# Turning mixing weights, head outputs and the normed context through the DMA's crossbar

## The chip, the core and the metric

The kernel runs on one core of one Trainium2 chip. The metric is the device time of one run in microseconds (us); before the change it is 1346.94 us, the median of three runs (1346.42 to 1347.75). The engines are TensorE (PE in the profile; its weight loads are PEld), VectorE (DVE), ScalarE (ACT), GpSimd (POOL) and SyncE (SP), which here only issues DMAs.

## The reference

The reference is a two-layer trunk over 256 context tokens and 256 latent tokens of width 1024, in float32. Layer 0 has a bidirectional chunkwise mLSTM as its token mixer, layer 1 a multi-head latent attention; behind each stands a gated feed-forward part with a convolution. Every part is modulated by the conditioning (scale and shift), and its output is added to the input and normed:

```python
h = x*(1+scale)+shift
x = LayerNorm(ALPHA*x + gate*sublayer(h))
# mLSTM of layer 0, 4 heads of 256 (q, k) and 512 (v), per direction and chunk:
wmat = jnp.exp(dmat - mj[..., None]) * jnp.einsum("bhjd,bhsd->bhjs", qc, kc)
num = g[..., None] * jnp.einsum("bhjd,bhde->bhje", qc, C) + jnp.einsum("bhjs,bhse->bhje", wmat, vc)
den = g * jnp.einsum("bhjd,bhd->bhj", qc, n) + jnp.sum(wmat, -1)
h = num / jnp.maximum(jnp.abs(den), jnp.exp(-mj))[..., None]
```

Each head's output is multiplied by an output gate, normed over its 512 columns (root mean square) and projected together with the others (the product called mout here).

## The kernel before, in words

**Matrix products.** A float32 product is made of three matmuls (`mm3`, lines 430, 433 and 434): each operand is split in a rounded high half, which ACT writes by a copy, and the remainder, its low half, which DVE writes by a subtraction (`split`, lines 444 and 445). The weights stream: SP loads 512 KB into `raw` (three buffers), ACT casts the high half of `w` (line 345), DVE subtracts for the low half (line 368), and PE multiplies from `w` (three buffers; some of the last weights of a product go to `wu`, from a larger pool).

**The mixer by heads.** Gates and all of v are there already: v in DRAM as `vd`, the output gates as `od`, the log decays as `ad`. For each head h from 0 to 3, `w_qk(h)` projects q and k (four column blocks of 128, each with 48 matmuls, and four casts `qk`), then `av(h-1)` multiplies the mixing weights of the head before with its v, and `s_mm(h)` makes the scores S of head h (`sc` and `sl` on PE, three copies `S` by ACT). Between the matmuls of `w_qk(h)` background generators advance a step at a time:

- `post(h-2)` norms the gated output `oh` of head h-2: four squares and a root on ACT, four scalings on DVE. Then PE turns the 16 blocks of 128x128 into `hnT` in PSUM, and ACT and DVE split each with its norm weight into `hn`.
- `head(h-1)` loads the decays of head h-1 over all partitions (`aB`, by POOL), adds the causal mask (`Am`, DVE), and makes the mixing weights W in three groups g of rows: exponentials on ACT, products with S, row sums and scalings on DVE. Then PE turns 12 blocks into `PT` in PSUM, and ACT and DVE split them.
- `v_load(h-1)`, called late in `w_qk(h)`, has POOL load v (`vr`) and the gate (`oh`), and has ACT and DVE split v.

A second background list computes the modulations of later parts (`ar` loads by SP, reductions on DVE of 1.2 us, called `junk` at line 544).

**mout and the norm.** After the loop mout runs over the 256 context tokens: the 16 blocks k of `hn` in turn, with `head(3)` and `post(2)` beside the first eight, then `av(3)`, then the others with `post(3)`. Its second pass, over the latent tokens, has the layer norm of the context rows beside it (`after0`): `ln_rows` norms two tiles `z` of 128x1024, and `ln_T` turns 16 blocks into `zT` in PSUM, modulates them (`zm`) and splits them into `h0`, the input of the feed-forward part.

**What sets the order.** The code's order, with the steps of the generators in between, is the starting point. When the kernel is built, a scheduler puts each engine's instructions in an order of its own, in which an instruction may pass others that it does not depend on; `behind` keeps an instruction after another one of its engine. A buffer is handed out from a pool (`s2`: 15 of 128x512, `u`: 31 of 128x1024), and the write into it waits until its former tile has been read. Each engine works through its list in order, so that an instruction that waits holds up everything behind it; SP and POOL issue DMAs in order, too.

Of the kernel before, what the change touches and what calls it, by code (L numbers as in the profile page):

```python
# [8 lines left out]
F32R = mybir.dt.float32r  # L9
I32 = mybir.dt.int32  # L10
AF = mybir.ActivationFunctionType
ALU = mybir.AluOpType
# [21 lines left out]
NB, NRAW, NU, NS = 3, 3, 31, 15  # L34
# [366 lines left out]
class K:  # L401
# [41 lines left out]
    def split(self, hi, lo, src):  # L443
        self.nc.scalar.copy(hi, src)
        self.nc.vector.tensor_sub(lo, src, hi)

    def smc(self, name):
# [593 lines left out]
    def head(self, h, S, big=False):  # L1041
        nc = self.nc
        aB = [self.s2("aB0"), self.s2("aB1")]
# [11 lines left out]
        P = []  # L1055
        for g in range(3):
            jbs = [0, 1] if g == 0 else [g + 1]
# [8 lines left out]
            for i, t in enumerate(jbs):  # L1066
                base = 256 * i if g == 0 else 0
                for d in range(2):
                    o = W[d]
                    bias = self.gcol[:, 0, t, 32 * d + h:32 * d + h + 1]  # L1070
# [28 lines left out]
            for i, t in enumerate(jbs):  # L1099
# [7 lines left out]
                                               op0=ALU.mult, op1=ALU.add)  # L1107
                P.append((W[big], b0))
            yield
        yield  # L1110
        self.PT = []
        for grp in ([(t, s) for s in range(2) for t in (0, 1)], [(t, s) for s in range(2) for t in (2, 3)],
                    [(t, s) for s in (2, 3) for t in (2, 3)]):
# [68 lines left out]

    def post(self, h, tt):
        nc = self.nc
# [6 lines left out]
        for t in range(4):  # L1191
            nc.vector.tensor_scalar(tt[t], tt[t], ss[:, t:t + 1], None, op0=ALU.mult)
        yield
        g = self.smc("mng")
        for e in range(4):
# [11 lines left out]
            self.hn[k] = u  # L1207
        yield


# [68 lines left out]
    def ln_T(self, zs, A, B, dst, tail, both=True, between={}):  # L1279

        nc = self.nc
        lone = both and tail
        for k0 in (0, 2, 6) if lone else range(0, 8, 2 if both else 4):
# [37 lines left out]
            for k in range(k0, k0 + n) if both else ():  # L1321
# [10 lines left out]
                if k % 2 or not tail:  # L1332
                    yield

    def aout_fin(self, o1, pl, xr, gate, fi, h1u, att):
# [846 lines left out]
def build(tc, off, a, out):  # L2182
    es = ExitStack()
    with es:
# [16 lines left out]
        tt = None  # L2201
        k.hn = {}
        for h in range(H0):
# [5 lines left out]
            if h >= 1:  # L2209
                gens.append(k.head(h - 1, S))  # L2210
            k.bg = gens
            k.w_qk(h, 2, (lambda: k.v_load(h - 1)) if h >= 1 else None)
# [6 lines left out]
        pc = k.acc4()  # L2219
        k.bg = [k.head(3, S, True), k.post(2, tt)]  # L2220
        vs = k.v_steps(3)
# [4 lines left out]
        tt = k.av(3)  # L2226
        k.bg = [k.post(3, tt)]
        k.outmm("mout", range(8, 12), hn, pc, 0, 16, 1, n2=ADA_M)
# [10 lines left out]
        def after0(pss, xr, gate, g, ln, l, c, dst, xdst):  # L2239
# [3 lines left out]
            zs = k.zs  # L2243
            yield from k.ln_T(zs, A, B, dst, g == 1)
            if xdst is not None:
# [117 lines left out]
```

## Time and profile before

| | before |
|---|---|
| median of three runs | 1346.94 us (1346.42 to 1347.75) |
| profiled execution: its span, the one time that its page gives | 1345.3 us |
| PE busy | 1334.9 us, 99% |
| DVE busy | 1059.0 us, 79% |
| ACT busy | 711.7 us, 53% |
| POOL busy | 141.5 us, 11% |
| chain of waits | 97% PE |
| DMA | 304.02 MB, mean 226 GB/s |

The span runs from the first to the last instruction that the profiler recorded. A row of the timeline gives start, duration, engine, line, operation, tile and inputs, and in brackets the idle time before it and who ended it. Rows of consecutive equal instructions are joined (x16): the duration is then that of all. A row of a tile's instructions gives the shortest, middle and longest duration in ns. A row of the DMA issues gives the size and the median time from issue to landing.

### The profile page before, as it was taken

Reading aid. Unit: us, or ns where it says so; the run is one execution under the profiler, and the core shown is the slowest. Engines: PE = TensorE matmul, PEld = TensorE weight load, DVE = VectorE, ACT = ScalarE, POOL = GpSimd, SP = SyncE. Lnnn points to the kernel's source line nnn. Section 1 sums busy time; section 2 is a strip of 40 time slices with the busy share of each in tenths; the row PEclk is TensorE's granted clock in tenths of the full one; section 3 lists DMA queues with packets and bytes.
Section 4 is the critical chain, followed back from the end, with each engine's and each line's share of the span. In section 5 each row is a group of like instructions: output and inputs, shape, how many; then the busy total and the mean of one; then the engine's idle time right before and its main releaser. Section 6 shows DMA issues by size and latency. Waiting matters only on the chain.

```text
span 1345.3 us, 18750 instructions
## 1 busy us (share of the span) xinstructions
PE 1334.9 (99%) x6659; PEld 1120.2 (83%) x6659; DVE 1059.0 (79%) x1745; ACT 711.7 (53%) x1252; POOL 141.5 (11%) x236
## 2 busy tenths in 40 slices
PE   9999999999999999999999999999999999999997
PEld 5777888888888888888898888888888998988886
DVE  4798656678688696897979977758899889898874
ACT  4765444445744546474644334333566767676660
POOL 0222000011101011020002011111000002000100
PEclk9999999999999999999999999999999999999999
DMA  9988848889686384776628989967866437376750
GB/s 364 330 277 279 281 163 248 233 272 307 235 281 230 102 255 149 228 292 222 215 86 261 328 260 286 282 181 184 300 223 194 157 104 219 127 212 189 263 189 32
DMA packets 99885, 304.02 MB, mean 226 GB/s; under 512 B 12312, under 2 KB 25112, under 8 KB 99712
## 3 DMA queue, kind: packets, MB, share of 16 engines
q1 hardware_dynamic: 62992, 218.65, 48.6%
q0 software_dynamic: 26000, 66.75, 17.9%
q10 hardware_dynamic: 10800, 17.44, 3.6%
q8 instruction: 52, 0.85, 0.3%
q14 instruction: 41, 0.34, 0.1%
HBM read 272.21 MB, written 42.12 MB: 234 GB/s over the span
## 4 chain that ended last, share of the span: by engine, by line
PE 97%; DMA 1%; DVE 1%; ACT 0%; issue 0%; SPq 0%; DVEq 0%; ACTq 0%
PE fin L1503 8%; PE tok L430 6%; PE tok L434 6%; PE tok L433 6%; PE fin L433 6%; PE fin L434 6%; PE y L433 6%; PE fin L430 6%; PE y L434 6%; PE y L430 6%; PE qk L430 4%; PE qk L433 4%; PE qk L434 4%; PE up L718 2%; PE up L430 2%; PE up L434 1%
## 5 line engine op out<-in xcount | busy, mean ns | idle before, releaser
L368 DVE TENSOR_TENSOR w<-raw,w 128x1024 fp32r<-128x1024 f32 (+2 forms) x286 | 343.2, 1203 | 131.9 <-ACT w L345 129.7
L345 ACT CAST w<-raw 128x1024 fp32r<-128x1024 f32 (+2 forms) x286 | 296.2, 1037 | 282.4 <-PE tok L434 77.8
L544 DVE SCALAR_TENSOR_TENSOR junk<-ar,bc 128x1024 f32<-128x1024 f32 x128 | 156.1, 1219 | 5.2 <-ACT bc L586 2.3
L433 PE MATMUL fin<-h,w 128*128 128x512 f32 (+1 forms) x370 | 139.6, 377 | 0.0
L430 PE MATMUL fin<-h,w 128*128 128x512 f32 (+1 forms) x370 | 139.5, 377 | 0.0
L434 PE MATMUL fin<-h,w 128*128 128x512 f32 (+1 forms) x370 | 139.3, 377 | 0.0
L1503 PE MATMUL fin<-h,w 128*128 128x512 f32 (+1 forms) x636 | 111.1, 337 | 0.0
L1503 PEld LDWEIGHTS fin<-h,w 128*128 128x128 f32 x636 | 97.6, 190 | 13.2
L430 PE MATMUL qk<-xc,w 128*128 128x512 f32 x256 | 100.2, 391 | 0.0
L434 PE MATMUL qk<-xc,w 128*128 128x512 f32 x256 | 99.8, 390 | 0.0
L433 PE MATMUL qk<-xc,w 128*128 128x512 f32 x256 | 99.6, 389 | 0.0
L433 PEld LDWEIGHTS fin<-h,w 128*128 128x128 f32 x370 | 69.6, 188 | 13.0
L430 PEld LDWEIGHTS fin<-h,w 128*128 128x128 f32 x370 | 69.6, 188 | 12.9
L434 PEld LDWEIGHTS fin<-h,w 128*128 128x128 f32 x370 | 69.6, 188 | 12.6
L434 PEld LDWEIGHTS qk<-xc,w 128*128 128x128 f32 x256 | 48.0, 188 | 10.1
L430 PEld LDWEIGHTS qk<-xc,w 128*128 128x128 f32 x256 | 48.1, 188 | 9.8
L433 PEld LDWEIGHTS qk<-xc,w 128*128 128x128 f32 x256 | 48.1, 188 | 9.8
L430 PE MATMUL tok<-w,hT 128*128 128x512 f32 x128 | 49.9, 390 | 0.0
L433 PE MATMUL tok<-w,hT 128*128 128x512 f32 x128 | 49.8, 389 | 0.0
L434 PE MATMUL tok<-w,hT 128*128 128x512 f32 x128 | 49.8, 389 | 0.0
L735 ACT ACTIVATE fg<-fg 128x512 f32<-128x512 f32 (+1 forms) x44 | 23.1, 525 | 50.0 <-DVE fg L733 43.9
L368 DVE TENSOR_TENSOR wu<-raw,wu 128x1024 fp32r<-128x1024 f32 (+1 forms) x37 | 43.8, 1203 | 3.5 <-ACT wu L345 3.2
(486 smaller groups left out, 3125.7 us busy)
## 6 DMA issues: line engine op xcount, KB each, us to landing
raw<-in_ws SPq DMA_DIRECT2D x282, 512.0 KB, 4.5
ar<-in_adaT SPq DMA_DIRECT2D x80, 512.0 KB, 6.0
t4d<-in_ws POOLq DMA_DIRECT2D x20, 512.0 KB, 9.1
adaw<-in_ada SPq DMA_DIRECT2D x16, 512.0 KB, 8.0
zr<-fd ACTq DMA_DIRECT2D x33, 128.0 KB, 4.6
xmd<-xr POOLq DMA_DIRECT2D x16, 256.0 KB, 4.4
xcd<-cv POOLq DMA_DIRECT2D x16, 256.0 KB, 4.9
xs<-xmd POOLq DMA_DIRECT2D x16, 256.0 KB, 6.0
```

The costliest lines, as they stand in the source:

```text
L345: self.cast = k.nc.scalar.copy(h[:, :cols], src)
L368: i = self.k.nc.vector.tensor_sub(l[:, :n], src, h[:, :n])
L430: q = mm(out, w[0], x[0], start=start, stop=False, skip_group_check=on)
L433: mm(out, w[0], x[1], start=False, stop=False, skip_group_check=on)
L434: mm(out, w[1], x[0], start=False, stop=stop, skip_group_check=on)
L544: nc.vector.scalar_tensor_tensor(o, w, 1.0, self.bc[j], op0=ALU.mult, op1=ALU.mult, accum_out=col[:, k, j:j + 1])
L718: nc.tensor.matmul(ps[m], wk[i][:, c], hT[k][:, j], start=made[m] == 0, stop=made[m] == 23)
L735: nc.scalar.activation(tmp[:, :n], tmp[:, :n], AF.Silu)
L1503: self.nc.tensor.matmul(ps[:, 0:256] if x else ps, w[x][:, k * 128:(k + 1) * 128], h[:, 0:256] if x else h, start=i == 0 and not k0, stop= ...
```

## The change

For heads 0 to 2 the blocks of W and of `oh`, and for the context rows those of `z`, are no longer turned on PE. ACT copies a tile into `pl` with the two 16-bit halves of each float32 in separate planes (`planes`), POOL writes `pl` to DRAM (`pd`, `hd`, `zd`), and SP issues transposing DMAs of 16-bit elements that read it and leave the turned float32 block in SBUF (`px`, `hx`, `zx`, 256 KB each). ACT and DVE then split from there. In numbers: 36 PE transposes of W, 48 of `oh` and 16 of `z` go; 26 copies on ACT, 26 writes by POOL and 25 transposing DMAs on SP come. `turn_heads`, a generator of its own, takes what `post` left in DRAM, one head later in the loop. Head 3 and the latent rows keep the PE transposes.

```diff
+    def planes(self, dst, src):
+        i = self.nc.scalar.copy(dst, src.bitcast(U16).rearrange("p (n h) -> p h n", h=2))
+        return i
...
     def head(self, h, S, big=False):
-        nc = self.nc
+        nc, last = self.nc, big
+        pd = None if last else self.dr.tile([512, 2, 512], U16, name="pd")
...
                 P.append((W[big], b0))
+            if not last:
+                n = 256 if g == 0 else 512
+                pl = self.pool.tile([128, 2, 512], U16, tag="s2", name="pl", bufs=NS)
+                for i, t in enumerate(jbs):
+                    p = pl if g else pl.rearrange("p a (b n) -> p (a b) n", b=2)[:, 2 * i:2 * i + 2]
+                    src, b0 = P[t]
+                    self.planes(p, src[:, b0:b0 + n])
+                    nc.gpsimd.dma_start(pd[t * 128:(t + 1) * 128, :, 0:n], p)
             yield
         yield
         self.PT = []
+        if not last:
+            v = pd.rearrange("t h n -> (t h) n")
+            for t0, s0 in ((0, 0), (2, 0), (2, 2)):
+                x = self.s2("px")
+                nc.sync.dma_start_transpose(x.bitcast(U16).rearrange("p (s t) -> p s t", s=2),
+                                            v[256 * t0:256 * t0 + 512, 128 * s0:128 * s0 + 256])
+                u = self.u("PT")
+                self.split(u[:, 0], u[:, 1], x)
+                self.PT.append(u)
+            yield
+            return
...
-    def post(self, h, tt):
+    def post(self, h, tt, last=False):
...
+        if not last:
+            d = self.dr.tile([512, 2, 512], U16, name="hd")
+            for t in range(4):
+                pl = self.pool.tile([128, 2, 512], U16, tag="s2", name="pl", bufs=NS)
+                self.planes(pl, tt[t])
+                nc.gpsimd.dma_start(d[t * 128:(t + 1) * 128], pl)
+            self.turned.append((h, d))
+            yield
+            return
...
+    def turn_heads(self):
+        nc, g = self.nc, self.smc("mng")
+        h, d = self.turned.pop(0)
+        v = d.rearrange("t h n -> (t h) n")
+        xs = []
+        for e in range(4):
+            x = self.s2("hx")
+            nc.sync.dma_start_transpose(x.bitcast(U16), v[:, e * 128:(e + 1) * 128])
+            xs.append(x)
+            if e % 2:
+                yield
+        for e in range(4):
+            k, x = h * 4 + e, xs[e]
+            u = self.u("hn")
+            nc.scalar.activation(u[:, 0], x, AF.Copy, scale=g[:, k:k + 1])
+            nc.vector.scalar_tensor_tensor(u[:, 1], x, g[:, k:k + 1], u[:, 0], op0=ALU.mult, op1=ALU.subtract)
+            self.hn[k] = u
...
+    def ln_turn(self, zs, A, B, dst):
+        nc = self.nc
+        d = self.dr.tile([256, 2, 1024], U16, name="zd")
+        for t in range(2):
+            pl = self.pool.tile([128, 2, 1024], U16, tag="u", name="pl", bufs=NU)
+            self.planes(pl, zs[t])
+            nc.gpsimd.dma_start(d[t * 128:(t + 1) * 128], pl)
+            pl = None
+            yield
+        v = d.rearrange("t h n -> (t h) n")
+        xs = []
+        for k in range(0, 8, 2):
+            x = self.s2("zx")
+            nc.sync.dma_start_transpose(x.bitcast(U16).rearrange("p (k t) -> p k t", k=2), v[:, 128 * k:128 * k + 256])
+            xs.append(x)
...
+            nc.scalar.activation(m, m, AF.Identity, bias=B[:, k:k + 1], scale=A[:, k:k + 1])
+            hi, lo = dst(k)
+            nc.scalar.copy(hi, m)
+            nc.vector.tensor_sub(lo, m, hi)
...
             if h >= 1:
                 gens.append(k.head(h - 1, S))
+            if h >= 2:
+                gens.append(k.turn_heads())
...
-    k.bg = [k.head(3, S, True), k.post(2, tt)]
+    k.bg = [k.head(3, S, True), k.post(2, tt), k.turn_heads()]
...
-            yield from k.ln_T(zs, A, B, dst, g == 1)
+            if g:
+                yield from k.ln_T(zs, A, B, dst, True)
+            else:
+                yield from k.ln_turn(zs, A, B, dst)
```

The new work also moves instructions that the diff does not name. The first piece is ACT's list in the second half of `w_qk(2)`, before the change, from the cast of the first `PT` of head 1 on; `vr` is v as loaded, `adav` a column of the background modulations.

```order
L444 CAST PT_4174<-PT_4169 128x512
L444 CAST PT_4182<-PT_4177 128x512
L444 CAST PT_4190<-PT_4185 128x512
L559 COPY adav_78<-w_4198 1x1
L444 CAST qk_4233<-qk_4139 128x512
L444 CAST v_4239<-vr_4237 128x512
L444 CAST v_4244<-vr_4242 128x512
L444 CAST v_4249<-vr_4247 128x512
L444 CAST v_4254<-vr_4252 128x512
L345 CAST w_4267<-raw_4013 128x1024
```

The same stretch with the change:

```order
L445 CAST PT_4167<-px_4165 128x512
L346 CAST w_4311<-raw_4077 128x1024
L565 COPY adav_78<-w_4311 1x1
L445 CAST PT_4172<-px_4170 128x512
L445 CAST PT_4177<-px_4175 128x512
L445 CAST qk_4228<-qk_4135 128x512
L346 CAST w_4426<-raw_4136 128x1024
L565 COPY adav_78<-w_4426 1x1 x2
L445 CAST v_4234<-vr_4232 128x512
L445 CAST v_4239<-vr_4237 128x512
L445 CAST v_4244<-vr_4242 128x512
L445 CAST v_4249<-vr_4247 128x512
```

The casts of v were directly behind `qk`; now a cast of a weight, `w_4426`, stands ahead of them. Its buffer is that of `w_4185`, the last weight that `w_qk(2)` reads. On DVE the low half of `w_4426` and one reduction stand ahead of v's first low half, too.

The second piece is POOL's list from `w_qk(1)` to `w_qk(2)`, before the change:

```order
L1662 DMA t4d<-in_ws 16x8192 x2
L1133 DMA vr<-vd 128x512 x4
L1139 DMA oh<-od 128x512 x4
L1045 DMA aB_3990<-ad 128x512
L1045 DMA aB_3991<-ad 128x512
```

and with it:

```order
L1750 DMA t4d<-in_ws 16x8192 x2
L1123 DMA pd<-pl 256x1x256 x2
L1123 DMA pd<-pl 128x1024 x2
L1159 DMA vr<-vd 128x512 x4
L1165 DMA oh<-od 128x512 x4
L1225 DMA hd<-pl 128x1024 x2
L1052 DMA aB_3975<-ad 128x512
L1225 DMA hd<-pl 128x1024 x2
L1052 DMA aB_3976<-ad 128x512
```

The loads `aB` of head 1 now stand between and behind the writes `hd` of head 0's output, and the loads of v and gate behind the writes `pd` of the mixing weights.

The third piece is ACT's list in the second pass of mout with the change, from the copy of the second normed tile on:

```order
L450 COPY pl<-z 128x2048
L346 CAST w<-raw 128x1024 x3
L1415 ACTIVATE zx<-zx,lnB,lnA 128x256 x2
L1417 CAST h_5546<-zx 128x256
L1417 CAST h_5547<-zx 128x256
L1415 ACTIVATE zx<-zx,lnB,lnA 128x256 x2
L1417 CAST h_5548<-zx 128x256
L1417 CAST h_5549<-zx 128x256
L346 CAST wu<-raw 128x1024
L1415 ACTIVATE zx<-zx,lnB,lnA 128x256
L346 CAST wu<-raw 128x1024
L1415 ACTIVATE zx<-zx,lnB,lnA 128x256
```

Before, the casts `wu` of the last mout weights had the modulations of `zm` ahead of them, which read PSUM; now they stand behind four modulations that read what the transposing DMAs bring.

More of the change, by code (lines that the diff above doesn't have):

```diff
@@ L10 @@
 I32 = mybir.dt.int32
+U16 = mybir.dt.uint16
 AF = mybir.ActivationFunctionType
@@ L1208, in post @@
         yield
+    def turn_heads(self):
[15 more added lines that the diff above has]
+            self.hn[k] = u
+            xs[e] = x = None
+            if e % 2:
+                yield
     def bcast(self, row, name):
@@ L1333, in ln_T @@
                     yield
+    def ln_turn(self, zs, A, B, dst):
[6 more added lines that the diff above has]
+            pl = None
+            yield
+        v = d.rearrange("t h n -> (t h) n")
[4 more added lines that the diff above has]
+            xs.append(x)
+            if k == 2:
+                yield
+        yield
+        for k in range(8):
+            if k % 2 == 0:
+                x = xs.pop(0)
+            m = x[:, k % 2 * 256:k % 2 * 256 + 256]
+            nc.scalar.activation(m, m, AF.Identity, bias=B[:, k:k + 1], scale=A[:, k:k + 1])
+            hi, lo = dst(k)
+            nc.scalar.copy(hi, m)
+            nc.vector.tensor_sub(lo, m, hi)
+            if k % 2:
+                x = m = None
+                yield
     def aout_fin(self, o1, pl, xr, gate, fi, h1u, att):
@@ L2201, in build @@
         tt = None
-        k.hn = {}
+        k.hn, k.turned = {}, []
         for h in range(H0):
@@ L2226, in build @@
         tt = k.av(3)
-        k.bg = [k.post(3, tt)]
+        k.bg = [k.post(3, tt, True)]
         k.outmm("mout", range(8, 12), hn, pc, 0, 16, 1, n2=ADA_M)
```

## The prediction

> **What bounds the kernel now.** I read the page first: its head, the table of engines and the chain of waits.
>
> ```profile
> span 1345.3 us, 18750 instructions
> PE 1334.9 (99%) x6659; PEld 1120.2 (83%) x6659; DVE 1059.0 (79%) x1745; ACT 711.7 (53%) x1252; POOL 141.5 (11%) x236
> PE 97%; DMA 1%; DVE 1%; ACT 0%; issue 0%; SPq 0%; DVEq 0%; ACTq 0%
> ```
>
> TensorE is busy 99% of the span and makes 97% of the chain. So whatever is taken from PE shortens the program by its own length, and whatever makes PE wait lengthens it one for one: there is no slack on PE to hide in. The span is 1345.3 us and the median of the runs 1346.94, so 1.6 us lie around the span; I sum against the span and add 1.6.
>
> Next the timeline of PE and the instructions of the three transposed tiles.
>
> ```profile
> L1118 PE MATMUL PT<-ident,W x48: 270/272/298, 417.3 to 595.6; 128*128 128x128 f32 x48
> L1198 PE MATMUL hnT<-ident,oh x64: 270/273/328, 465.1 to 616.9; 128*128 128x128 f32 x64
> 465.06 2.03 PE L1198 MATMUL hnT<-ident,oh 128*128 128x128 f32 x16
> 466.85 0.48 PE L430 MATMUL qk<-xc,w 128*128 128x512 f32 x1
> 467.17 0.40 PE L433 MATMUL qk<-xc,w 128*128 128x512 f32 x1
> 487.39 1.47 PE L1118 MATMUL PT<-ident,W 128*128 128x128 f32 x12
> 488.62 0.47 PE L430 MATMUL qk<-xc,w 128*128 128x512 f32 x1
> ```
>
> **The gain.** The change takes 3 x 12 PT, 3 x 16 hnT and 16 zT transposes off PE, 100 in all. A single one's 272 ns overlaps its neighbours, so I price from start to start: 16 take 466.85 - 465.06 = 1.79 us, 12 take 1.23, about 0.10 to 0.11 each. The matmul behind a group also starts its successor late (466.85 to 467.17 is 0.32 where the others are 0.23 apart): 0.1 a group. In ten groups the 100 make 100 x 0.102 + 10 x 0.1 = 11.2 us (10 to 12.5). If everything that replaces them were hidden, the span would be 1334.1.
>
> **What replaces them.** Per tile now: an ACT copy that separates the two 16-bit halves, a POOL write to DRAM, a crossbar transpose issued by SP, then the split by ACT and DVE as before. 25 transposes of 256 KB, 26 writes, 26 copies. The copies hold 128x512 to 128x2048; for 128x1024 there are casts, 1.04 us each (first row):
>
> ```profile
> L345 ACT CAST w<-raw 128x1024 fp32r<-128x1024 f32 (+2 forms) x286 | 296.2, 1037 | 282.4 <-PE tok L434 77.8
> raw<-in_ws SPq DMA_DIRECT2D x282, 512.0 KB, 4.5
> xmd<-xr POOLq DMA_DIRECT2D x16, 256.0 KB, 4.4
> od<-o ACTq DMA_DIRECT2D x16, 256.0 KB, 2.4
> vd<-v POOLq DMA_DIRECT2D x16, 256.0 KB, 6.7
> vr<-vd POOLq DMA_DIRECT2D x16, 256.0 KB, 4.7
> z<-x1d POOLq DMA_DIRECT2D x4, 512.0 KB, 6.2
> ```
>
> ACT gains about 27 us of work on 711.7 of 1345, which the PE time covers; without that cover it would cost its 27. The DVE count is unchanged. Bytes: some 13.5 MB on 304, covered likewise except where windows are full (context LN, below). What isn't covered is latency: a 256 KB write lands after 2.4 to 6.7 us, of which I take 4.4 (same size and queue, SBUF to DRAM); no row shows a crossbar transpose, so I bound it by the quickest 256 KB row (2.4) and twice the vr row (9.4) and take 4.7, that of a 256 KB load. The way from W or oh to PT or hn gets a copy, a write and a read: 1.0 + 4.4 + 4.7 = about 10 us, where PE needed 1.2 to 1.8.
>
> **Heads 1 and 2.** PE must start av when the projection w_qk of the next head ends. Before, w_qk(2) ran from 458.20 to 505.05, with this in it (rows of the four engines' timelines):
>
> ```profile
> 458.20 0.39 PE L430 MATMUL qk<-xc,w 128*128 128x512 f32 x1
> 464.79 0.40 ACT L1087 ACTIVATE W<-Am,gcol 128x128 f32<-128x128 f32 x1
> 484.79 0.74 DVE L1105 SCALAR_TENSOR_TENSOR W<-W,R 128x512 f32<-128x512 f32 x1
> 494.85 2.18 ACT L444 CAST v<-vr 128x512 fp32r<-128x512 f32 x4
> 499.80 1.05 ACT L345 CAST w<-raw 128x1024 fp32r<-128x1024 f32 x1 [1.51 <-PE qk L434]
> 495.59 2.49 DVE L445 TENSOR_TENSOR v<-vr,v 128x512 fp32r<-128x512 f32 x4
> 505.05 0.39 PE L430 MATMUL av<-v,PT 128*128 128x512 f32 x1
> 420.94 1.04 PE L1118 MATMUL PT<-ident,W 128*128 128x128 f32 x8
> ```
>
> The last mixing weight is done at 485.5, and v is ready at 498, seven microseconds ahead of av. The change without its 16 + 12 transposes makes av due at about 505.05 - 1.9 - 1.3 = 501.8.
>
> What is late in its place: first the decays. POOL now issues the two aB loads behind the writes of the head before (second order piece above), and each write waits for its copy, which waits for the norm of the head before.
>
> ```profile
> 463.18 0.30 ACT L1189 ACTIVATE ss<-ss,keps 128x4 f32<-128x4 f32 x1
> 422.28 0.54 POOL L1045 DMA_DIRECT2D aB<-ad  x1 [3.55 <-PE PT L1118]
> 488.29 0.54 POOL L1045 DMA_DIRECT2D aB<-ad  x1 [12.76 <-PE PT L1118]
> DMA to landing us min/median/max: 4.5/6.6/7.3
> ```
>
> Before, the loads for heads 1 and 2 went out at 422.28 and 488.29, a whole stage early; the last row is aB's own landing. Now: the norm's root is done at 463.5, a weight cast and four copies end at about 468.7, the second aB load goes out behind them at 469 and lands 6.6 later, 475.6; Am takes 0.7. So W starts at 476.3 instead of 464.8. From the first W row to the end of the last, 20.7 us passed before, with DVE full; order puts about as much between the two now (six background reductions, three weight splits, the W work). That gives 497 for the last mixing weight. If the background work ran in the wait instead, the W work alone is some 8 us: 484, no later than before.
>
> From 497: copy 1.0, write 4.4, transpose 4.7: 507. Then ACT's order decides (first order piece): three PT and qk casts, the weight cast, and only then v. About 3.4 us to v's high half, and on DVE the weight split 1.2, a reduction 1.2 and v's low half 0.7 from the weight cast on: 513. PE waits 513 - 501.8 = 11.2 us.
>
> Lower bound: with transfers that land at once there is still the weight cast that ACT holds ahead of v, and it waits for the last matmul of w_qk, since the three weight buffers are in use. PE then waits 1.05 + 1.22 + 1.22 + 0.69 = 4.2 us (weight cast, split, reduction, v's low half). Upper bound: a 6.7 write and a 9.4 transpose, 18. Head 2 repeats it in w_qk(3), with the same order. Head 0 has aB early and its W done by 421 (the last row); ten microseconds more still lie well before its av, at the end of w_qk(1) near 445: nothing. So 2 x 11.2 = 22.4 us (8 to 36).
>
> **Mout.** Head 2's outputs are turned during av(3):
>
> ```profile
> 598.46 1.91 PE L1198 MATMUL hnT<-ident,oh 128*128 128x128 f32 x16
> 597.38 1.26 DVE L1192 TENSOR_SCALAR oh<-oh,ss 128x512 f32<-128x512 f32 x3
> 609.77 0.39 PE L430 MATMUL y<-w,hn 128*128 128x512 f32 x1
> ```
>
> The first y behind av needs them, due at 609.77 - 1.9 = 607.9. oh is scaled by 598.6, four copies end at 601, the write lands at 605.4, the transposes at 610.1, hn takes 0.7 + 0.7: 611.5. Wait 3.6, I take 4 (0 to 9).
>
> **Context norm ahead of the FFN.** Two copies (2 x 1.04 each), two 512 KB writes, four transposes, while the weights of mout still stream:
>
> ```profile
> 648.31 0.82 ACT L1261 ACTIVATE z<-z,nm,rs 128x512 f32<-128x512 f32 x1
> 649.03 1.00 ACT L1326 ACTIVATE zm<-zT,lnB,lnA 128x256 f32<-128x256 f32 x2
> 649.92 0.70 ACT L1330 CAST h<-zm 128x256 fp32r<-128x256 f32 x2
> 662.99 1.05 ACT L345 CAST w<-raw 128x1024 fp32r<-128x1024 f32 x1 [1.45 <-DMA raw<-in_ws]
> 650.00:665.00 15.00, 15.00 (x71) 12.38 (x71) 12.77 (x17) 12.97 (x22) 1.61 (x3) 1.00 0.91 305
> 665.32 0.39 PE L430 MATMUL y<-wu,hn 128*128 128x512 f32 x1
> ```
>
> In the row of the window 650 to 665 the queues (its last two numbers are the DMA's share and GB/s) are at 0.91 of their share and ACT waits for a load already. z is there at 649.1, the copy ends at 651.2, the write lands at 657.4 (6.2), the transposes at about 662.5. ACT has four modulations and four casts of them (4 x 0.50 + 4 x 0.35 = 3.4 us, the rows of zm and h) ahead of the wu cast that PE needs (third order piece): 667.0 with the cast. It is due at 665.32 - 1.5 = 663.8: a wait of 3.2, with the low half 4 (1 to 9).
>
> **Sum.** 1345.3 - 11.2 + 22.4 + 4 + 4 = 1364.5 of span, 1366 as a run's time.
>
> A rule speaks against the change as such. The Trainium skill, "VectorE: DVE Perf Modes", section "Rules for kernel authors", says to turn a 128x128 block on TensorE where its result may lie in PSUM, and to leave the crossbar for other cases; its table of the three paths has 1309 ns for a block by crossbar. No run here shows that figure yet; by it, eight blocks one after another (my estimate) are 10.5 us for a 256 KB transpose, and the sum, with 5.8 more at each of the four places, would be near 1390. The series rival below is its mechanism.
>
> **Rivals.**
>
> *All hidden*: 1345.3 - 11.2 + 1.6 = 1335.7. PE's share speaks for it, ACT's place for v's casts behind a weight cast that waits for PE's last projection speaks against it. Chance 0.08.
>
> *Only the order bites*: background work fills the wait for aB, writes land like od in 2.4, and what remains are 4.2 for each of two heads, 0 in mout and 1 at the norm: 1345.3 - 11.2 + 9.4 + 1.6 = 1345. Chance 0.2, half of it faster, a quarter the same.
>
> *Transposes in series*: SP's four transposes of a group follow one another at 4.7 each rather than together. Heads 1 and 2 (two late ones): +4.7 each; mout and norm (four): +14 each: 1404. It decides as soon as one transpose takes longer than its share of a load. Against it: 512 KB loads of SP land in 4.5 and overlap. Chance 0.12.
>
> *The clock falls at each wait*, so each wait costs a stretch at half pace. What the trace has on it is the start:
>
> ```profile
> 1.49 3.78 PE L655 MATMUL idle<-zero 128*128 128x512 f32 x8 [1.49 <-DVE adav L497]
> ```
>
> Eight matmuls at 0.47 each, where the projection's are 0.23 apart: 2 us lost. Four long waits would add some 2.2 each: 1375. Against it: nothing in this trace shows PE idle later on. Chance 0.15. The Trainium skill, "TensorE: Matmul & The Clock Gate", section "What's actually happening", has this as a rule: an idle window of about 3.4 us halves the clock until a busy one of the same length; by it my waits of 11 us would do it and the trace's start agrees with half pace.
>
> **How the numbers follow.** The sum above has 0.45, all hidden 0.08, order only 0.2, series 0.12, clock 0.15. The forecast's own range is 1352 to 1384; to hold 8 in 10 it takes in most of the order-only and clock cases and stops short of the series one: 1342 to 1392. A measurement tells about 0.2% (2.7 us) from no change. Faster: 0.08 + 0.10, same 0.05 + 0.02 of the forecast, slower the rest, 0.75.
>
> **What would show it.** Right: PE idle of 4 to 18 us ahead of av for heads 1 and 2, ended by v (ACT or DVE) or PT; W of these heads starting over 5 us later than before after the start of w_qk; no idle ahead of head 0's av; waits of a few us at the first y behind av(3) and at the first wu matmul of mout. Wrong: PE still at 99% and a span near 1334 (all hidden); waits of 4 us alone (order only); transposes landing 10 us and more after issue, one by one (series); a granted clock well under 1 behind each wait (clock).

## The result and the profile after

The kernel with the change takes 1394.62 us (1393.66 to 1395.69, four runs) against 1346.93 (1346.42 to 1347.75) for the kernel before on the same chip: 1.0355 times as long, with a 95% interval of 1.0342 to 1.0369. The forecast was 1366 us with a range of 1342 to 1392: slower was right, the size was not. The profiled execution has a span of 1392.8 us, 47.5 more than before.

The head of the page after, its table of engines, the clock and the chain:

```profile
span 1392.8 us, 18696 instructions
PE 1335.5 (96%) x6559; PEld 1115.8 (80%) x6559; DVE 1058.4 (76%) x1745; ACT 737.0 (53%) x1278; POOL 156.7 (11%) x262
PEclk9999999999999979897999999999999999999999
PE 78%; issue 14%; DMA 4%; POOL 1%; ACT 1%; DVE 1%; SPq 0%; DVEq 0%; POOLq 0%
```

The row of the clock on the page before (the span in 40 slices; a 9 is 90% or more of the full clock):

```profile
PEclk9999999999999999999999999999999999999999
```

The 100 transposes are gone (6659 PE instructions are 6559), yet PE is busy as long as before, and the clock, flat before, dips in the middle. TensorE lost 19 points of the chain. Whom PE waited for, from the view of waits (total, times, longest):

```profile
PE av L431 <- ACT v L445: 27.9, 2, 14.2
PE y L431 <- ACT hn L1260: 14.4, 1, 14.4
PE y L431 <- ACT wu L346: 3.6, 1, 3.6
PE av L434 <- DVE v L446: 1.4, 1, 1.4
```

These are the places that the prediction named: av of heads 1 and 2, the first y behind av(3), the first `wu` matmul. With the last, 0.5 for a second `wu` tile, they make 47.8 us. With the 11.2 us at which the prediction priced the transposes, the span should have grown by 36.6; it grew by 47.5. The other 11 are in the pace of PE behind each wait. Here is PE around av(1) on the timeline of the kernel after (start, length, engine, line, operation, in brackets the wait ahead of it):

```profile
514.42 0.79 PE L431 MATMUL av<-v,PT 128*128 128x512 f32 x1 [14.15 <-ACT v L445]
516.59 0.79 PE L434 MATMUL av<-v,PT 128*128 128x512 f32 x1 [1.38 <-DVE v L446]
517.18 0.63 PE L435 MATMUL av<-v,PT 128*128 128x512 f32 x1
517.61 1.05 PE L431 MATMUL av<-v,PT 128*128 128x512 f32 x2
518.46 0.67 PE L434 MATMUL av<-v,PT 128*128 128x512 f32 x1
518.93 0.63 PE L435 MATMUL av<-v,PT 128*128 128x512 f32 x1
```

And the table of windows of the same kernel around it (window, length, busy time of PE, PEld, DVE, ACT and POOL, then the granted clock, which is the share of its full speed that TensorE was given, the DMA engines' share and GB/s):

```profile
500.00:504.00 4.00, 0.26 (x2) 0.00 (x0) 3.06 (x4) 1.32 (x3) 2.93 (x6) 1.00 1.01 400
504.00:514.00 10.00, 0.00 (x0) 0.00 (x0) 2.42 (x4) 3.10 (x7) 0.00 (x0) 0.53 1.07 278
514.00:521.00 7.00, 5.21 (x11) 3.60 (x12) 7.00 (x12) 4.85 (x9) 0.00 (x0) 0.50 0.99 310
521.00:527.00 6.00, 6.00 (x26) 4.88 (x25) 3.93 (x8) 0.00 (x0) 0.00 (x0) 0.95 0.15 58
```

Some 4.3 us into the wait the granted clock falls to a half (PE's last matmul ends at 500.3, and 0.53 over the ten microseconds from 504 puts the fall at 504.6). It stays there for 7.2 us after PE has work again (0.95 from 521 to 527 puts the return at 521.6): the matmuls run 0.43 apart (517.18 to 517.61, 518.46 to 518.93 is 0.47) where w_qk's are 0.23 apart. So this wait costs some 3 us more than its length: 7.2 us without the 1.4 of waiting in them are 5.8 us of work at half pace, of which 2.9 are not done.

The same in mout and at the first `wu` (table of windows of the same kernel, same columns):

```profile
649.00:655.00 6.00, 5.03 (x12) 4.03 (x13) 2.26 (x3) 3.75 (x8) 1.07 (x2) 0.52 1.08 178
710.00:712.00 2.00, 1.54 (x3) 0.94 (x4) 1.78 (x2) 2.00 (x4) 0.28 (x1) 0.50 1.01 375
```

PE works at half pace for 5.8 us at av(1), 4.6 at av(2) (588.6 to 593.3), 4.7 in mout (650.0 to 654.7) and 5.7 at `wu` (710.0 to 716.2): 20.8 us in all. Half of that, 10.4, is work not done, and it makes all but half a microsecond of the 11.

What made av(1) late, from the timelines of DVE, POOL, SP and ACT:

```profile
495.60 0.75 DVE L1112 SCALAR_TENSOR_TENSOR W<-W,R 128x512 f32<-128x512 f32 x1
497.72 0.54 POOL L1123 DMA_DIRECT2D pd<-pl  x1 [2.04 <-DVE w L369]
498.55 2.24 POOL L1159 DMA_DIRECT2D vr<-vd  x4 [0.29 <-issue]
500.78 1.08 POOL L1165 DMA_DIRECT2D oh<-od  x2
502.36 5.77 SPq L1131 DMA_TRANSPOSE px<-pd  x2
510.51 0.62 ACT L445 CAST PT<-px 128x512 fp32r<-128x512 f32 x1 [9.16 <-DMA px<-pd]
513.75 2.17 ACT L445 CAST v<-vr 128x512 fp32r<-128x512 f32 x4
```

Up to 502.36 this is the forecast almost to the half microsecond: last mixing weight at 496.3, write landed 4.6 us after its issue. From there the transposing read takes 8.2 us and not 4.7 (502.36 to 510.51), while the DMA engines are full (a share of 1.01 and 400 GB/s up to 504, 1.07 up to 514): v and gate, 2 MB that POOL now issues behind the last write, go through in the same stretch, and SP adds four hx transposes at 508.2.

In mout the same thing is larger (timelines of POOL, SP and ACT):

```profile
631.35 2.19 POOL L1654 DMA_DIRECT2D xres<-in_tok  x4 [0.17 <-issue]
633.02 18.07 SPq L1253 DMA_TRANSPOSE hx<-hd  x4
634.58 0.54 POOL L1272 DMA_DIRECT2D gate<-gd  x1
649.20 0.72 ACT L1260 ACTIVATE hn<-hx,sm 128x512 fp32r<-128x512 f32 x1 [17.53 <-DMA hx<-hd]
```

The first of the four transposes of head 2's outputs is issued at 633.02, and ACT can read it at 649.2, 16.2 us later; SP is busy with the four issues for 18 us (2.1, 8.1, 5.5 and 2.1). The loads of the residual, `xres`, stand on POOL behind the writes of these outputs. Before, they began 9 us ahead of av(3) (592.6 against 601.6); now they begin 4.7 us behind its start (631.35 against 626.68), and so beside the transposes.

### The profile page after: what moved, and what is told of

Same layout as the page of the kernel before. It is cut to its first block, busy times and chain, and to the rows that moved or that the text cites. A ratio compares the mean times of both kernels' runs of the same rounds, so it can differ in the third digit from the quotient of the medians.

```text
span 1392.8 us, 18696 instructions
## 1 busy us (share of the span) xinstructions
PE 1335.5 (96%) x6559; PEld 1115.8 (80%) x6559; DVE 1058.4 (76%) x1745; ACT 737.0 (53%) x1278; POOL 156.7 (11%) x262
## 2 busy tenths in 40 slices
DMA packets 128302, 317.14 MB, mean 228 GB/s; under 512 B 39128, under 2 KB 51928, under 8 KB 128128
## 4 chain that ended last, share of the span: by engine, by line
PE 78%; issue 14%; DMA 4%; POOL 1%; ACT 1%; DVE 1%; SPq 0%; DVEq 0%; POOLq 0%
PE fin L1591 8%; PE tok L431 6%; PE tok L435 6%; PE tok L434 6%; PE fin L434 6%; PE fin L435 6%; PE fin L431 6%; PE y L434 4%; PE y L435 4%; PE y L431 4%; PE up L724 2%; PE up L431 1%; PE up L435 1%; PE up L434 1%; PE y L1434 1%
## 5 line engine op out<-in xcount | busy, mean ns | idle before, releaser
L431 PEld LDWEIGHTS qk<-xc,w 128*128 128x128 f32 x256 | 48.0, 188 | 10.1
L431 PE MATMUL y<-w,hn 128*128 128x512 f32 x92 | 36.6, 403 | 14.4 <-ACT hn L1260 14.4
```

The source lines that it names most:

```text
L431: q = mm(out, w[0], x[0], start=start, stop=False, skip_group_check=on)
```

## The experiments

Three kernels each undo one part. First the mixing weights, on PE again:

```diff
-        nc, last = self.nc, big
+        nc, last = self.nc, h not in ()
```

> The mixing weights of heads 0 to 2 are turned on PE again (36 transposes, 3.9 us); head outputs and context rows stay with the crossbar. Theory A (px ends the waits ahead of av): these fall from 14 us each to 0 to 3, with the half pace behind them, and the run takes 1360 to 1366 us. Rival B (late aB and POOL's list alone make av wait): waits of 5 us and more stay, over 1370.

Measured: 1374.21 us, 1.0205 times before (1.0188 to 1.0221). The waits for v are gone, and two others stand there (waits of this kernel):

```profile
PE y L431 <- ACT hn L1260: 15.9, 1, 15.9
PE PT L1144 <- DVE W L1112: 8.2, 2, 4.5
```

PE now waits 4.5 and 3.7 us for W itself: the late W costs that much even with the quick way behind it (the second `aB` of head 1 still lands at 478.1). The time lies above theory A's 1360 to 1366, on the side of the rival (over 1370), the waits just above the one (0 to 3) and below the other (5 and more): px ended the waits for v, and behind it stands the late W.

Then the outputs, on PE again:

```diff
-                gens.append(k.post(h - 2, tt))
+                gens.append(k.post(h - 2, tt, h - 2 not in ()))
...
-            if h >= 2:
+            if h >= 2 and h - 2 in ():
...
-        k.bg = [k.head(3, S, True), k.post(2, tt), k.turn_heads()]
+        k.bg = [k.head(3, S, True), k.post(2, tt, True)]
```

(The last argument of `post` and `last` in the edit before send a head's blocks through PE.)

> The outputs of heads 0 to 2 are turned on PE again (48 transposes, 5.2 us); mixing weights and context rows stay with the crossbar. Theory A: the wait of 14.4 us in mout is gone, aB is early again, and the waits ahead of av fall from 14 to 3 to 7 each: 1358 to 1368 us. Rival B (av's waits do not depend on the outputs' way): they stay at 12 to 14 and the run at 1379 to 1385.

Measured: 1368.05 us, 1.015 (1.0135 to 1.0166), the upper end of what theory A gave.

```profile
PE av L431 <- ACT v L445: 14.9, 2, 8.3
```

With `aB` early again the two waits ahead of av halve (6.6 and 8.3), and mout's is gone. So the outputs' way is the dearest part, 26.6 us, half of it through what it does to the next head's mixing weights.

Then the context rows, on PE again:

```diff
-            if g:
-                yield from k.ln_T(zs, A, B, dst, True)
-            else:
-                yield from k.ln_turn(zs, A, B, dst)
+            yield from k.ln_T(zs, A, B, dst, g == 1)
```

> Only the context rows ahead of the feed-forward part are turned on PE again (16 transposes, 1.7 us). Theory A: PE's wait of 4.1 us at the first wu matmul goes, and the slow stretch behind it: 1388 to 1391 us. Rival B (the stage is short of DMA anyway and another wait takes its place): 1393 to 1396.

Measured: 1394.05 us (1391.69 to 1400.18), 1.0354 (1.0333 to 1.0376): no difference from the change that can be told. The wait for `wu` is gone, and others grew in the profiled execution:

```profile
PE av L431 <- ACT v L445: 30.4, 2, 16.8
PE y L431 <- ACT hn L1260: 18.2, 2, 17.0
```

The time is the rival's, its reason is not shown: the waits that grew lie ahead of this stage, in parts that the edit does not touch. This part is worth little either way, and the landings ahead of it vary by more than that.

The next ones ask why the reads land late. Plain reads of the same bytes:

```diff
-            nc.sync.dma_start_transpose(x.bitcast(U16), v[:, e * 128:(e + 1) * 128])
+            nc.sync.dma_start(x.bitcast(U16), d[e * 128:(e + 1) * 128].rearrange("t h n -> t (h n)"))
```

(px and zx likewise, and `planes` copies without separating the halves.)

> The transposing reads of px, hx and zx are replaced by plain reads of the same bytes from the same DRAM tiles (the blocks are not turned, and the copy ahead of the writes does not separate the halves, so the values are not the reference's); copies, writes, waits and buffers stay. Theory A (the crossbar's small packets make a 256 KB transpose land late): px and hx land after 4 to 6 us instead of 8.3 and 7.2 in the middle and 16.1 at most, PE's waits ahead of av fall from 14 to about 10 or 11, the one in mout from 14.4 to 5 to 8, and the run takes about 1377 us. Rival B (the round through DRAM and the places in the engines' lists make the wait, transposing or not): the waits stay within 1 us each, 1392 to 1396 us.

Measured: 1376.29 us, 1.0217 (1.0202 to 1.0232), the time of theory A, but not its mechanism: px still landed after 6.2 to 9.2 us and hx after 8.0 to 11.2, and the wait in mout is gone. These reads take rows of one written tile each and could start before the last write had landed, which the transposes could not. The second form takes rows of all of them:

```diff
-            nc.sync.dma_start_transpose(x.bitcast(U16), v[:, e * 128:(e + 1) * 128])
+            nc.sync.dma_start(x.bitcast(U16), d.rearrange("(p q) h n -> p q (h n)", q=4)[:, e])
```

> As the first plain-read kernel (blocks not turned, halves not separated), but each plain read now takes rows of all the tiles that the transposing DMA took, in pieces of 2 KB (512 B for head group 0), so that it may start no earlier than that did. Theory A (in the heads the landing is late because v, gates and weights are loaded at the same time; in mout the four transposes are slow by themselves beside the loads): the waits ahead of av stay at 11 to 15 us each, the wait in mout falls from 14.4 to 4 to 9: 1380 to 1388 us. Rival B (the crossbar is what is late everywhere): the waits ahead of av fall to 10 and less each, under 1378. Rival C (it is the way through DRAM alone): no wait falls by more than 2, 1391 to 1396.

Measured: 1380.4 us, 1.0242 (1.0226 to 1.0258). The waits of this kernel:

```profile
PE av L431 <- ACT v L445: 25.5, 3, 13.7
PE y L431 <- ACT hn L1261: 7.3, 1, 7.3
```

Ahead of av plain reads are nearly as late as transposing ones: the waits are 13.7 and 11.7 (the third is 0.1) against 14.2 and 13.8, and for heads 1 and 2 px lands after 6.7 to 7.6 us against 7.7 to 9.0. In mout they halve the wait: the first hx is used 8.8 us after its issue instead of 16.2. So theory A, in the main: in the heads the crossbar makes the smaller part of the lateness, some 2 us a wait.

What else is on the queues? First mout, with the loads of residual and gate for the context rows left out:

```diff
-                    self.nc.gpsimd.dma_start(x, src[t0 + t][:, c])
+                    self.nc.gpsimd.memset(x, 0.0) if t0 == 0 else self.nc.gpsimd.dma_start(x, src[t0 + t][:, c])
...
-        gate = k.bcast(k.gd[0, 2][1:2, :], "gate")
+        gate = [k.s2("gate") for _ in range(2)]
+        for t in gate:
+            nc.gpsimd.memset(t, 1.0)
```

> The loads of xres and gate for the context rows, 1.5 MB that POOL issues while head 2's outputs are turned ahead of mout's ninth block, are left out (the tiles are set to constants on POOL, so the residual and the gate of the context rows are missing). Theory A (the transposes share the DMA engines with these loads, and get the smaller part): the first hx of that group lands in 6 to 9 us instead of 16.1, PE's wait in mout falls from 14.4 to 5 to 8, the run takes 1385 to 1389 us. Rival B (four transposes are slow by themselves, at some 80 to 100 GB/s): the wait stays above 12 us and the run at 1392 to 1395.

Measured: 1397.65 us, 1.0376 (1.036 to 1.0391). That is above both theories. The wait came in two pieces, 4.8 and 7.0, with 2.5 behind them, as long as before in sum. It looked like rival B, but the edit did not do what it was meant to: POOL issued the four residual loads of the latent rows at once in the place that had become free (636 to 638), so the queues were still shared. The first hx, issued ahead of these loads, was used 6.7 us after its issue, as theory A has it; the others landed after 16 to 18 us. The next one holds back all of them:

```diff
-            self.nc.gpsimd.dma_start(t, row[:, h * 512:(h + 1) * 512].to_broadcast([128, 512]))
+            i = self.nc.gpsimd.dma_start(t, row[:, h * 512:(h + 1) * 512].to_broadcast([128, 512]))
+            if name == "gate":
+                self.tc.keep_in_program_order(i)
...
+                    if t0 == 0 and not t and not h and 11 in self.hn:
+                        self.nc.gpsimd.tensor_copy(x[:, 0:1], self.hn[11][:, 0, 0:1].bitcast(F32))
-                    self.nc.gpsimd.dma_start(x, src[t0 + t][:, c])
+                    self.tc.keep_in_program_order(self.nc.gpsimd.dma_start(x, src[t0 + t][:, c]))
```

> POOL's loads of xres and gate for both passes of mout wait until head 2's outputs are turned and split (one column of the first is copied into the first tile ahead of its load), so that the four transposes of that group have the DMA engines almost to themselves; everything is computed. Theory A (sharing makes them late): the first lands 4 to 8 us after its issue instead of 16.1, PE's waits for hn in mout fall from 14.4 to 5 to 9 in all, 1386 to 1391 us if the held loads are still in time. Rival B (four transposes are slow by themselves): waits above 12, 1393 or more.

Measured: 1385.44 us, 1.0284 (1.027 to 1.0298), 9 us off the change and just under theory A's 1386 to 1391. The wait of this kernel in mout:

```profile
PE y L431 <- ACT hn L1260: 5.2, 1, 5.2
```

The landing of hx in this kernel, from the view of that tile (the trace has it for four of the twelve transposes, one of head 0's and three of mout's):

```profile
DMA to landing us min/median/max: 3.7/4.0/6.4
```

The same row of the kernel with the change (the same four):

```profile
DMA to landing us min/median/max: 4.4/7.2/16.1
```

Theory A: with the queues free of these loads none of the four lands later than 6.4 us, the first of mout's is used 6.5 us after its issue, and PE waits 5.2, close to the 4 that were forecast. So 9 of the 14.4 us in mout come from the loads that ran beside the transposes; held back, these were still in time (no wait of PE for them).

Now the heads. `aB` ahead of the writes of the head before:

```diff
+    def decays(self, h):
+        self.aBn = [self.s2("aB0"), self.s2("aB1")]
+        for d in range(2):
+            i = self.nc.gpsimd.dma_start(self.aBn[d], self.ad[d, h:h + 1, :].to_broadcast([128, 512]))
+            self.tc.keep_in_program_order(i)
...
-        aB = [self.s2("aB0"), self.s2("aB1")]
-        for d in range(2):
-            nc.gpsimd.dma_start(aB[d], self.ad[d, h:h + 1, :].to_broadcast([128, 512]))
+        aB = self.aBn
...
+            if h >= 1:
+                k.decays(h - 1)
             if h == 0:
                 gens.append(k.gate_chain())
...
+        k.decays(3)
```

> POOL issues the two aB loads of each head ahead of the writes of the head before, nothing else is moved in the code. Theory A (the late aB makes the mixing weights late, as the prediction had it): W of heads 1 and 2 is done 8 to 11 us earlier relative to the start of w_qk, PE's waits ahead of av fall from 14 to 4 to 6 each, and the run takes 1375 to 1379 us. Rival B (the wait is set by the turned outputs or by SP's list of transposes): the waits stay above 11 us and the run above 1389.

Measured: 1384.77 us, 1.0278 (1.0259 to 1.0298), between the theories. The waits of this kernel:

```profile
PE av L431 <- ACT v L445: 19.2, 2, 10.1
PE y L431 <- ACT hn L1264: 14.4, 1, 14.4
```

W is done earlier, as theory A has it: 31.1 us after the start of w_qk for both heads, where it was 39.8 and 38.0. But the waits fall from 14 to 9.1 and 10.1, not to 4 to 6: for head 1 the last write took 6.6 us instead of 4.6 and the read behind it 9.9 instead of 8.2, and px landed after up to 12.3 us in this kernel. `aB` is 4 to 5 us of each wait, and write and reads took the rest back. Next, v and gate are loaded earlier as well (VE names the column block of the projection at which they are):

```diff
-VE = {1: (3, 0), 2: (3, 0), 3: (3, 0)}
+VE = {1: (1, 0), 2: (1, 0), 3: (1, 0)}
```

> aB is issued ahead of the writes of the head before, and v and gate of a head are loaded a quarter to half a projection earlier, ahead of pd on POOL. Theory A (late aB, and the loads of v and gate that share the DMA engines with px, make up the waits ahead of av): px lands after 4 to 7 us, and the waits fall from 14 to 0 to 5 each, with less of the half pace behind them: 1364 to 1374 us. Rival B (px is late by itself): the waits stay at 9 us as with aB alone, 1381 or more.

Measured: 1393.35 us, 1.0342 (1.0328 to 1.0356). For heads 1 and 2 px now lands after 4.2 to 4.4 us, since v and gate are through by then, and of the wait for v 0.3 us is left. But the time is hardly better than the change's:

```profile
PE y L431 <- ACT hn L1264: 15.7, 1, 15.7
PE av L431 <- ACT PT L445: 12.3, 4, 5.0
```

Half of theory A is there: the reads are quick once the loads are out of their way. The other half is not. The casts of v, which wait for their loads (ACT waits up to 3.9 us ahead of one; the last is at 481.5), now stand on ACT ahead of the exponentials of W, the first of which is at 483.5. So W is late again: that of head 1 is done 44.2 us after the start of w_qk(2), later than with the change (39.8) and than with `aB` alone (31.1). The waits of the heads came down from 29 to 18 us, in smaller pieces (12.3, and 5.9 ahead of the scores); the stretch from av(3) to the first feed-forward matmul grew by 2.5, and the half pace came back behind the small pieces. Moving loads earlier in lists that are worked through in order moves the waits.

The pace: matmuls without use, 58 ahead of av(1) and av(2) and ahead of mout's ninth block.

```diff
             ps = self.ps("av")
+            if t == 0 and h in (1, 2):
+                for _ in range(58):
+                    q = nc.tensor.matmul(ps, self.xc[0][:, 0, 0:128], self.xc[0][:, 0], start=True, stop=True)
+                    self.tc.keep_in_program_order(q)
...
+        ps = k.ps("idle")
+        x = k.hn[0]
+        for _ in range(58):
+            q = nc.tensor.matmul(ps, x[:, 0, 0:128], x[:, 0], start=True, stop=True)
+            k.tc.keep_in_program_order(q)
```

> 58 matmuls without use (13.2 us at full pace) stand ahead of the first av of heads 1 and 2 and ahead of mout's ninth block, where PE waited 14.2, 13.8 and 14.4 us. Theory A (PE's pace halves because it idles, some 2.7 us lost behind each wait): the granted clock stays at 1.00 there, av's first matmuls run 0.23 apart instead of 0.43, and the run takes 1386 to 1388 us. Rival B (the slow matmuls come from full DMA queues or late operands): they stay 0.43 apart and the run takes 1394 us or more.

Measured: 1397.52 us (1393.53 to 1406.81), 1.0393 (1.0349 to 1.0437). Its time is the rival's; its timeline speaks for theory A. PE in mout, on the timeline of this kernel:

```profile
638.66 13.31 PE L2324 MATMUL idle<-hn 128*128 128x512 f32 x58
651.80 0.39 PE L431 MATMUL y<-w,hn 128*128 128x512 f32 x1
652.03 0.39 PE L434 MATMUL y<-w,hn 128*128 128x512 f32 x1
```

The table of windows of this kernel, same columns as before:

```profile
638.00:652.00 14.00, 14.00 (x63) 11.62 (x62) 0.75 (x1) 1.90 (x4) 2.15 (x4) 1.00 1.07 280
```

Kept busy, PE has a clock of 1.00 with the DMA engines at 1.07 of their share, and y runs 0.23 apart from its first matmul on, where it ran 0.43 apart in the kernel of the change. So the half pace comes from PE's idling, and not from full queues or late operands. From the end of av(3) to the first feed-forward matmul this kernel is 2.8 us shorter than the change (88.7 against 91.5). At the heads v came 1.1 to 1.2 us later in this execution, PE idled for a few us behind the 58, and part of the half pace returned: from the end of w_qk to the end of av the two heads took 0.8 and 2.3 us longer, which is as much as mout won.

Last, a kernel that keeps the crossbar only where there is room: the mixing weights of head 0, the outputs of heads 0 and 1, and `aB` first (decays as above).

```diff
-        nc, last = self.nc, big
+        nc, last = self.nc, h not in (0,)
...
-        aB = [self.s2("aB0"), self.s2("aB1")]
-        for d in range(2):
-            nc.gpsimd.dma_start(aB[d], self.ad[d, h:h + 1, :].to_broadcast([128, 512]))
+        aB = self.aBn
...
-                gens.append(k.post(h - 2, tt))
+                gens.append(k.post(h - 2, tt, h - 2 not in (0, 1)))
...
-            if h >= 2:
+            if h >= 2 and h - 2 in (0, 1):
...
-        k.bg = [k.head(3, S, True), k.post(2, tt), k.turn_heads()]
+        k.decays(3)
+        k.bg = [k.head(3, S, True), k.post(2, tt, True)]
...
-            if g:
-                yield from k.ln_T(zs, A, B, dst, True)
-            else:
-                yield from k.ln_turn(zs, A, B, dst)
+            yield from k.ln_T(zs, A, B, dst, g == 1)
```

> Only what has room stays with the crossbar: the mixing weights of head 0 and the outputs of heads 0 and 1 (44 transposes off PE), with aB issued ahead of the writes; the rest is turned on PE as before. Theory A (a turn through the crossbar is free where 15 us of slack lie behind it): PE never waits, 1346.9 - 44 x 0.105 = 1342 us, 1341 to 1344. Rival B (copies, writes and SP's transposes slow the weight stream or v): 1346 or more.

Measured: 1344.42 us (1342.72 to 1345.87, 11 runs) against 1347.28 (15 runs): 0.9977 (0.9968 to 0.9986), faster than the kernel before by 2.9 us, and than the change by 50. Theory A, with 1342, holds but for 2 us; 1.3 of them are a wait in its own list of waits:

```profile
PE sc L434 <- DVE qk L446: 1.3, 1, 1.3
```

With v and gate loaded earlier on top:

```diff
-VE = {1: (3, 0), 2: (3, 0), 3: (3, 0)}
+VE = {1: (1, 0), 2: (1, 0), 3: (1, 0)}
```

> Mixing weights of head 0 and outputs of heads 0 and 1 by the crossbar, all else on PE, aB ahead of the writes, and v and gate loaded earlier. Theory A (the 1.3 us wait ahead of the scores in the first such kernel and its other small losses come from crowding late in the projection): 1342 to 1344 us. Rival B (copies and transposes cost their part elsewhere): 1344 to 1347.

Measured: 1356.43 us, 1.0066 (1.0054 to 1.0079), worse than either theory. The largest wait of this kernel:

```profile
PE PT L1148 <- DVE W L1116: 10.0, 4, 4.0
```

and ACT's first exponential of head 1's W, on the timeline of this kernel:

```profile
483.74 0.70 ACT L1098 ACTIVATE W<-Am,gcol 128x128 f32<-128x128 f32 x2
```

The casts of v wait for their loads on ACT with the exponentials of W behind them: the first W of head 1 begins at 483.7 here, at 470.8 without this edit and at 464.8 before.

## Why the prediction was right or wrong

**Direction and places: right.** Slower, with waits ahead of av(1), av(2), behind av(3) and at the first `wu`, none ahead of av(0). Each was there and had the releaser that was named.

**The gain: right.** The stretch from the start of w_qk(1) to that of w_qk(2), where nothing waits, fell from 57.2 to 55.9 us for 12 transposes, 0.11 each.

**Late `aB`, late W: right, the times in part by luck.** Second Am at 476.2 (forecast 476.3), last W at 496.3 (497), write landed in 4.6 (4.4). But the second `aB` went out at 467.9 instead of 469 and took 8.3 us instead of 6.6; the two errors cancel. The kernels with `aB` first and with W on PE put its price at 4 to 5 us a head.

**The transposing read, "take 4.7, that of a 256 KB load": wrong.** This is the step that failed, and its upper bound with it. A read was priced by the middle of a load over the whole program, but it is issued where the transfers that the same change moved are in flight. It took 8.2 us in w_qk(2) and 9.0 in w_qk(3) (plain reads took 6.9 and 6.7 there), and 16.2 in mout, above the 9.4 that I had as an upper bound. The heads' waits came to 15.5 and 13.8 instead of 11.2 each, mout's to 14.4 instead of 4; with these loads held back mout waited 5.2, and with v and gate out of the way px landed after 4.2 to 4.4 us.

A smaller error sits in the heads' sum: av of head 1 was due at 500.3 and not at 501.8. I took the 16 + 12 transposes of w_qk(2) off and forgot the twelve of head 0 in w_qk(1), so that w_qk(2) starts 1.6 us earlier (456.6 against 458.2).

**Context norm: right,** 4.1 against 4, again by two errors that cancel: the write took 8.0 us instead of 6.2, the read 3.5 instead of 5.1.

**The clock: a term, not a rival.** This is the second step that failed: the sum has nothing for it. I had it as a case of its own at 0.15, to add 9 us; it happened on top of the waits and added 11. With waits of 11 us in the sum, the program's own start at half pace should have put it into the sum. The Trainium skill, "TensorE: Matmul & The Clock Gate", section "What's actually happening", has windows of about 3.4 us for both ways; the trace agrees on the fall (4.3 us into the wait) and has the return later than one window, 7.2 us after av(1) began, with 1.4 us of further waiting in it.

1345.3 - 11.2 + 15.5 + 13.8 + 14.4 + 4.1 + 10.9 = 1392.8, the span measured; the 10.9 is what is left over, and the stretches at half clock hold 10.4 of it. Of the 28.3 us between forecast and span (1364.5 and 1392.8), mout's wait has 10.4, the clock 10.9 and the heads' waits 6.9.

**The series rival** (four transposes one after another): not as stated. In mout its sign was there, hx landing late and one by one (ACT reads them at 649.2, 651.4, 652.4 and 654.7), but with the loads beside them held back the last is read 4.2 us behind the first, and none came more than 6.5 us after its issue. When nothing else was going, four zx were issued 1.3 us apart and the first was used 3.5 us after its issue (timelines of SP and ACT of the kernel with the change):

```profile
702.22 5.29 SPq L1406 DMA_TRANSPOSE zx<-zd  x4
705.67 1.09 ACT L1415 ACTIVATE zx<-zx,lnB,lnA 128x256 f32<-128x256 f32 x2 [6.33 <-DMA zx<-zd]
```

Nor does the prediction's estimate by the Trainium skill, "VectorE: DVE Perf Modes", section "The three transpose paths" (1309 ns for a block, eight in a row, 10.5 us), hold here: 3.5 us for a tile of eight. That its 1390 comes near the time measured is chance. **All hidden** and **only the order bites** did not come about. That the first holds for the mixing weights of head 0 and the outputs of heads 0 and 1, but for 2 us, is what the faster kernel shows.

What stays open: why a transpose is so much later than a plain read beside the loads in mout (16.2 us against 8.8). Plain reads (7.3) and held loads (5.2) each took half or more of the wait away; the two were not tried together. Nor was a kernel tried that has every cure at once, so that part of the heads' waits is explained and not removed.

## What to carry to other kernels

When work goes from a busy engine to the DMA, price its latency at the place and time where it is issued, with what the same edit moves there: read the DMA share of that window, and list what stands on POOL's and SP's queues beside it. On a kernel whose TensorE is full, add to a wait of 14 us some 2 to 3 us for the halved clock behind it. Move only what has a whole stage of slack, and check what the moved instructions push back on every queue: here 44 of the 100 transposes were worth moving, with `aB` issued first; with the other 56, and `aB` late, the gain of 3 us became a loss of 48.

## What was not expected of the hardware

A transposing DMA keeps SP busy for 1.25 us and more, where a plain one takes 0.33 in the middle, and up to 8.1 us when the queues are full; four in a row held SP for 18 us (the row of hx above). In w_qk(2) the next weight loads stood behind two px and four hx on SP, from 502.4 to 514.4. SP's rows for px and hx in the view of instructions of the kernel with the change (count: shortest, middle and longest in ns, first and last start):

```profile
L1131 SPq DMA_TRANSPOSE px<-pd x9: 1233/1344/5979, 421.6 to 577.4; - x9
L1253 SPq DMA_TRANSPOSE hx<-hd x12: 1242/1672/8139, 508.2 to 649.0; - x12
```

It moves in small pieces: packets under 512 bytes rose from 12312 to 39128, and the second kernel with plain reads has 13128, so that the 25 transposes make some 1040 each, for 256 KB. Alone it is quick (3.5 us), as the Trainium skill, "Advanced Engine Details and Errata", section "X-Bar Transpose (TRN2)", has it, by which a transposing DMA is as fast as a plain one; beside other loads in mout it was not: 16.2 us from issue to first use, against 8.8 for a plain read of the same bytes.
